# Groups of four transposes of the identity among the up-projections, and conditioning sums that are no longer kept back for the layer norms

## The chip, the cores and the metric

The kernel runs on one core of one Trainium2 chip. Its metric is the device time of one execution in microseconds (us); less is better. The core has a matmul engine (TensorE, PE in the profile, with its weight loads as PEld), two engines for elementwise work that read the matmul results (VectorE, DVE, and ScalarE, ACT), a slower general engine (GpSimd, POOL) and an engine that here only issues transfers (SyncE, SP). Each engine works through its own instructions in order and waits for the others by semaphores.

## What is computed

Two decoder layers over 256 positions of width 2048. Each layer has a token mixer (forgetting attention in layer 0, sliding-window attention in layer 1) and a gated feed-forward network (FFN) with a short convolution. Each sub-layer is scaled, shifted and gated by vectors that come from one conditioning vector `c`:

```python
c_act = jax.nn.silu(c)
for i in range(DEPTH):
    mod = c_act @ ada_w[i] + ada_b[i]
    sh1, sc1, g1, sh2, sc2, g2 = jnp.split(mod[:, None, :], 6, axis=-1)
    h = x * (1.0 + sc1) + sh1
    y = fox_attention(h, ...) if i % 2 == 0 else swa_attention(h, ...)
    x = layer_norm(DEEPNORM_ALPHA * x + (1.0 + g1) * y, ln_mix_g[i], ln_mix_b[i])
    h = x * (1.0 + sc2) + sh2
    y = conv_ffn(h, ffn_w_up[i], ffn_conv_w[i], ffn_conv_b[i], ffn_w_down[i])
    x = layer_norm(DEEPNORM_ALPHA * x + (1.0 + g2) * y, ln_ffn_g[i], ln_ffn_b[i])
```

`conv_ffn` multiplies `h` by `w_up` (2048 x 11264), convolves each channel over three positions, takes `silu(g) * val` of the two halves, and multiplies by `w_down` (5632 x 2048).

## The kernel before

**Weights.** All matrices are f32 in memory. `stream` (L256) walks over one block of 512 columns of a matrix, two chunks of 128 rows at a time: SP fetches a pair (512 KB), ACT rounds it to `wh` (L264), DVE takes the rest `wl = w - wh` (L275), and `go` (L266) issues the matmuls of the pair, then one `tick` of the background work. The activations are split in the same way into `hH` and `hL`, and each product is made of three matmuls: high by high, high by low, low by high.

**Two forms of matmul.** `w_stationary` (L326) is used for the up-projection and for query and key: the weights are the stationary operand and 256 positions stream past them, so each matmul has 256 columns; the profile names its output `ws`. One call has 8 pairs of 24 matmuls, 192 in all, that add up in two PSUM banks. `x_stationary` is used for the rest (`xs` in the profile, 512 columns a matmul).

**The FFN** (`conv_ffn`, L1053) works on the 11 blocks of 512 channels in two stages, `sbs = [(0, 6), (6, NB)]` (L1090): the up-projections of blocks 0 to 5 (two `w_stationary` calls a block, gate half and value half, so 12 calls), the down-projections that they feed, then blocks 6 to 10 (10 calls) and theirs. There are thus four up-projection stages in the two layers.

**Conditioning vectors in the background.** A list (L363) of ten vectors `(layer, v)` is worked off while the matmuls run: (0,3), (0,2), (0,4), (0,5), (1,0), (1,1), (1,3), (1,2), (1,4), (1,5). `ada_vector` (L369) is a generator; `tick` pays for its steps by a rate that is set for each stage. 32 steps each fetch a piece of `ada_w` and add it, times one element of `c`, to the tile `acc` (L391, L393). What then follows depends on the kind of vector:

- Gates (v = 2, 5) first load a bias row into `acc` by a POOL transfer (L381), and end in matmuls against ones (one of 512 columns for each bank) and ACT copies (L405).
- Shifts and scales end in four groups of four transposes of `acc` against the identity (L431), each group followed by four ACT instructions that sum the columns (L435), one group a step.
- The scales (0,4) and (1,4) stand in the table `HELD`. They keep their sums back: `held` collects two functions, and `release` (L444) runs them in the next layer norm, 16 short matmuls of one column against ones and one DVE instruction (L417).

After v = 4 no further vector is begun until `release` has cleared the flag `ada["held"]`.

**The layer norms between sub-layers.** `between` (L1120) runs where one sub-layer's last residual is finished and the next matrix needs the normalised, scaled and transposed `x`. `residual` (L615) has added the gated output and gathered the moments: for each half of the positions DVE prepares the variance (L630), and POOL raises it to the power -1/2 (L631). `between` then ran either `release` or, where nothing was held (the layer norm between the layers), `spin(o, 3)`: three matmuls of the identity by a constant of 384 columns, whose result nobody reads (L504). After that `modulate` (L509) queues the normalisation (L641 on ACT, L643 on DVE), the transposes of `x` (L482) with the scaling that writes `hH` and `hL` (L492 to L497), two further spins, and the first matmuls.

**Order.** The framework orders each engine's instructions by its own plan of when they will be ready; `pin` keeps an instruction in the order of the program. POOL's three instructions around a held layer norm come, in its queue, as L631, L381 (the bias row of the next gate), L631.

Of the kernel before, what the change touches and what calls it, by code (L numbers as in the profile page):

```python
# [17 lines left out]
P = 128  # L18
# [3 lines left out]
KC = D // P  # L22
# [7 lines left out]
DFF = 5632  # L30
# [6 lines left out]
WB = 512  # L37
# [4 lines left out]
def hybrid_trunk(ctx: ExitStack, tc: tile.TileContext, a: dict, out: bass.AP):  # L42
    nc = tc.nc
# [12 lines left out]
    def wtile(name="w"):  # L56
        return wp.tile([P, 2, WB], F32, tag="w", name=name)

    def gtile(name="g"):
        return gp.tile([P, 2, S], F32R, tag="g", name=name)  # L60

    def ttile(name="t"):
        return tp.tile([P, 2 * S], F32, tag="t", name=name)

    def bank(name="sm"):
        return psp.tile([P, 512], F32, tag="ps", name=name)

    def w_banks():
        return [bank("ws").rearrange("p (a s) -> p a s", a=2) for _ in range(2)]
# [4 lines left out]
    def mm(o, lhsT, rhs, start=False, stop=False, **kw):  # L74
        return nc.tensor.matmul(o, lhsT, rhs, start=start, stop=stop, **kw)  # L75

    def pin(ins, on=True):

        if on:
            tc.keep_in_program_order(ins)  # L80

    def split(h, l, src):

        nc.scalar.copy(h, src)  # L84
        nc.vector.tensor_tensor(l, src, f32(h), op=ALU.subtract)
# [14 lines left out]
    ident = cst.tile([P, P], F32, name="ident")  # L100
# [110 lines left out]
    def then(fn, alone=False):  # L211

        if alone:
            lone.add(fn)
        work.append(fn)
        if len(work) == 1 and not ahead[0]:
            settle()
# [3 lines left out]
    def settle(left=0):  # L221
        while work and (ahead[0] > left or not left):
            f = work.pop(0)
            rest(f, *work)
            f()
# [17 lines left out]
    def defer(gen):  # L243

        post.append(gen)

    def run_post():
        for g in list(post):
            if next(g, post) is post:
                post.remove(g)  # L250
# [5 lines left out]
    def stream(wsrc, row0, col, ks, use):  # L256

        for kc in ks[::2]:
            r0 = (row0 + kc) * P
            w = wtile()  # L260
            pin(nc.sync.dma_start(w, wsrc[r0:r0 + 2 * P, col:col + WB].rearrange("(k p) f -> p k f", p=P)), False)
            h = hl.tile([P, 2, WB], F32R, tag="wh", name="wh")
            l = hl.tile([P, 2, WB], F32R, tag="wl", name="wl")
            pin(nc.scalar.copy(h, w), False)  # L264

            def go(kc=kc, h=h, l=l):  # L266
                ahead[0] -= 1
                run_post()
                use(kc, h, l)
                if feeds:  # L270
                    feeds.pop(0)()
                tick()

            def residual_(w=w, h=h, l=l, go=go):
                pin(nc.vector.tensor_tensor(l, w, f32(h), op=ALU.subtract), behind[0] > 0)  # L275
                behind[0] -= 1
                del residuals[go]

            ahead[0] += 1
            weights.add(go)  # L280
            residuals[go] = residual_
            work.append(go)
            settle(2)
# [25 lines left out]
    def w_mm(ps, kc, h, l, last=KC - 1, first=0):  # L309

        for i in range(2):
            for f in range(4):
                o = ps[f // 2][:, f % 2, :]
                wh, wl = h[:, i, f * P:(f + 1) * P], l[:, i, f * P:(f + 1) * P]
                mm(o, wh, hH[:, kc + i, :], start=kc + i == first and f % 2 == 0, skip_group_check=True)
                mm(o, wh, hL[:, kc + i, :], skip_group_check=True)
                mm(o, wl, hH[:, kc + i, :], stop=kc + i == last, skip_group_check=True)
# [5 lines left out]
        stream(wsrc, k0, col, list(range(nk)), use)  # L323
        return ps

    def w_stationary(wsrc, col):  # L326

        ps = w_banks()
        stream(wsrc, 0, col, list(range(KC)), lambda kc, h, l: w_mm(ps, kc, h, l))
        return ps  # L330


# [18 lines left out]
    def drain():  # L351
        while bg["wait"] or bg["run"]:
            step()

    def tick():
        ada_tick()
        if not feeds:
            step()
# [5 lines left out]
    ada = {"gen": None, "debt": 0.0, "rate": 0.0, "gate_free": True}  # L364

    held = []
    HELD = {(0, 4): False, (1, 4): False}

    def ada_vector(l, v):  # L369
        row = v % 3 == 2  # L370
        if (l, v) in HELD and HELD[l, v]:
            q = [cst.tile([P, 512], F32, tag=f"ha{i}", name="ha") for i in range(4)]
# [47 lines left out]

        if (l, v) in HELD:
            held.append((sums, finish))
            ada["held"] = not HELD[l, v]
            ready_cols.add((l, v))
# [19 lines left out]
    def release():  # L444

        for s_, _ in held:
            s_()
        for _, f_ in held:
            f_()
        held.clear()  # L450
        ada["held"] = False
# [15 lines left out]
    def ada_need(l, v):  # L467
        while (l, v) not in cols and (l, v) not in gates and (l, v) not in ready_cols:
            ada_step()
# [34 lines left out]
    def spin(o, n):  # L504

        for _ in range(n):
            pin(mm(o[:, :3 * P], ident, mask.rearrange("p a b -> p (a b)"), start=True, stop=True))
# [545 lines left out]
    def conv_ffn(l):  # L1053
        w_up, w_dn = a["ffn_w_up"][l], a["ffn_w_down"][l]
        NB = DFF // WB
        cw = lambda j, f: ccol[:, l, j, f:f + 1]

        def conv(pf, f):
            u = tp.tile([P, S], F32, tag="u", bufs=3, name="u")
            nc.scalar.activation(u, pf, AF.Identity, bias=cw(CW, f), scale=cw(2, f))  # L1060
            nc.vector.scalar_tensor_tensor(u[:, 1:], pf[:, :S - 1], cw(1, f), u[:, 1:],  # L1061
                                           op0=ALU.mult, op1=ALU.add)
            nc.vector.scalar_tensor_tensor(u[:, 2:], pf[:, :S - 2], cw(0, f), u[:, 2:],  # L1063
                                           op0=ALU.mult, op1=ALU.add)
            return u

        def evac(ps, f0, then):
            u = None
            for f in range(5):
                v = conv(ps[f // 2][:, f % 2, :], f0 + f) if f < 4 else None  # L1070
                if u is not None:
                    then(f - 1, u)
                u = v
                yield
                yield

        def silu(sil):
            def f_(f, u):
                nc.scalar.activation(sil[f // 2][:, (f % 2) * S:(f % 2 + 1) * S], u, AF.Silu)
            return f_  # L1080

        def gated(sil, gT):
            def f_(f, u):
                nc.vector.tensor_tensor(u, u, sil[f // 2][:, (f % 2) * S:(f % 2 + 1) * S], op=ALU.mult)
                g = gtile("gT")
                split(g[:, 0, :], g[:, 1, :], u)
                gT.append(g)
            return f_

        sbs = [(0, 6), (6, NB)]  # L1090
        for si, (b0, b1) in enumerate(sbs):
            gT = []
            then(lambda: ada.update(rate=(0.64, 0.4)[l]))
            for b in range(b0, b1):
                ps = w_stationary(w_up, b * WB)
                sil = [ttile("sil") for _ in range(2)]
                then(lambda ps=ps, b=b, sil=sil: defer(evac(ps, b * 4, silu(sil))))
                ps = w_stationary(w_up, DFF + b * WB)
                then(lambda ps=ps, b=b, sil=sil, gT=gT: defer(evac(ps, DFF // P + b * 4, gated(sil, gT))))

            def stat(kc, t, gT=gT):
                while kc >= len(gT):
                    run_post()
                return gT[kc][:, 0, t * P:(t + 1) * P], gT[kc][:, 1, t * P:(t + 1) * P]

            def ready(si=si):
                if si == 0:
                    drain()
                ada_need(l, 5)
                ada["rate"] = (0.78, 0.4)[l]  # L1110

            then(ready)
            for d in range(D // WB):
                ps = x_stationary(w_dn, d * WB, b0 * 4, (b1 - b0) * 4, stat, (2, 4)[l] if si > 0 and d == D // WB - 1 else 0)
                then(lambda ps=ps, d=d, si=si: defer(residual(ps, d, gates[l, 5], si == len(sbs) - 1)),
                     si > 0 and d == D // WB - 1)
        then(lambda: (flush(), ada.update(gate_free=True)), True)


    def between(l, v, g, b, name, ll):  # L1120

        ada_need(l, v)
        ada_need(l, v + 1)
        o = bank("spin")
        if held:
            release()
        else:
            spin(o, 3)
        modulate(*merged(l, v, g, b, ll), normalise, o)
        behind[0] = 2  # L1130
        later([affine(name, ll)])
# [45 lines left out]
```

## Time and profile before

| what | value |
| --- | --- |
| time before, median of 3 runs | 2258.78 us (2256.72 to 2261.77) |
| profiled execution, its time | 2251.43 us |
| its span (first to last instruction) | 2249.7 us |
| mean granted TensorE clock | 0.989 |
| matmuls on PE | 14903 |
| of these `ws` (weights stationary) | 9984 |
| groups of four transposes of `acc` (L431) | 16 |

The profiled execution lies 7.35 us below the median of the runs. All durations come from it. A matmul's recorded duration is longer than the distance from its start to the next one's start, since matmuls are pipelined; the distances between starts are what counts. In a timeline row, the first number is the start, the second the duration of the row, the last the count of instructions merged into it, and in brackets stands the idle time of the engine and what ended it.

### The profile page before, as it was taken

To read this page: it belongs to the slowest core of one execution; us is meant where nothing else is said; L and a number is where in the kernel's file an instruction comes from. 1 tells how busy PE (TensorE), PEld (TensorE's weight loads), DVE (VectorE), ACT (ScalarE), POOL (GpSimd) and SP (SyncE) were. 2 spreads that over 40 slices of the span, in tenths; PEclk is the share of its full clock that TensorE was granted. 3 is DMA by queue.
4 is the path that set the end of the run, shared out by engine and by line. 5 is a ranking of instruction groups with operands and counts; after the bars stand their busy time and mean duration, and the time that the engine had idled before them with its cause. 6 is when DMAs were issued, how large, how long until landed. Compare 5 with 4: busy or idle time off the path is not lost. (4 is left out here: it accounts for less than half of the span.)

```text
span 2249.7 us, 38317 instructions
## 1 busy us (share of the span) xinstructions
PE 2199.5 (98%) x14903; PEld 2020.0 (90%) x14903; DVE 1793.5 (80%) x2450; ACT 1165.5 (52%) x1833; POOL 22.9 (1%) x52
## 2 busy tenths in 40 slices
PE   6999999999999999999999999999999999999997
PEld 6999888789999888999987888889999888999986
DVE  6979999979979978789799888779787555665656
ACT  3435656455555443655535588655555533454532
POOL 0000000000000000000000000000000000000000
PEclk9999999999999999999999999999999999999998
DMA  9999999959979989799797767559777556555553
GB/s 340 381 342 362 353 354 326 331 197 331 345 248 316 331 282 333 250 314 316 268 326 271 260 236 249 190 171 308 260 263 249 179 192 195 187 188 186 185 193 111
DMA packets 274246, 602.98 MB, mean 268 GB/s; under 512 B 21062, under 2 KB 29960, under 8 KB 273552
## 3 DMA queue, kind: packets, MB, share of 16 engines
q1 hardware_dynamic: 273008, 595.85, 77.2%
q0 software_dynamic: 1056, 4.69, 0.6%
q8 instruction: 116, 1.90, 0.3%
q14 instruction: 66, 0.54, 0.1%
HBM read 598.37 MB, written 2.10 MB: 267 GB/s over the span
## 5 line engine op out<-in xcount | busy, mean ns | idle before, releaser
L264 ACT CAST wh<-w 128x1024 fp32r<-128x1024 f32 x728 | 764.1, 1051 | 826.2 <-PE ws L75 291.8
L75 PE MATMUL ws<-hH,wh 128*128 128x256 f32 x6656 | 1177.6, 281 | 4.6 <-ACT hH L84 2.1
L275 DVE TENSOR_TENSOR wl<-w,wh 128x1024 fp32r<-128x1024 f32 x728 | 886.7, 1221 | 345.8 <-ACT wh L264 336.1
L75 PEld LDWEIGHTS ws<-hH,wh 128*128 128x128 f32 x6656 | 1020.7, 190 | 12.5 <-issue 4.8
L75 PE MATMUL ws<-hH,wl 128*128 128x256 f32 x3328 | 929.4, 281 | 3.6 <-DVE wl L275 3.5
L75 PEld LDWEIGHTS ws<-hH,wl 128*128 128x128 f32 x3328 | 632.5, 191 | 4.9 <-DVE wl L275 4.8
L75 PE MATMUL xs<-wh,gT 128*128 128x512 f32 x1408 | 435.6, 390 | 0.0
L75 PEld LDWEIGHTS xs<-wh,gT 128*128 128x128 f32 x1408 | 264.3, 188 | 54.6
L75 PE MATMUL xs<-wl,gT 128*128 128x512 f32 x704 | 273.9, 389 | 0.0
L75 PE MATMUL xs<-wh,hH 128*128 128x512 f32 x704 | 235.3, 400 | 0.1
L393 DVE SCALAR_TENSOR_TENSOR acc<-wa,cact,acc 128x1024 f32<-128x1024 f32 x180 | 228.1, 1275 | 0.0
L393 DVE SCALAR_TENSOR_TENSOR acc<-wa,cactp,acc 128x1024 f32<-128x1024 f32 x128 | 162.2, 1276 | 0.0
L75 PEld LDWEIGHTS xs<-wl,gT 128*128 128x128 f32 x704 | 132.2, 188 | 27.2
L75 PEld LDWEIGHTS xs<-wh,hH 128*128 128x128 f32 x704 | 131.4, 189 | 27.6 <-issue 1.0
L75 PE MATMUL xs<-wl,hH 128*128 128x512 f32 x352 | 139.5, 397 | 2.0 <-DVE wl L275 2.0
L1060 ACT ACTIVATE u<-ws,ccol 128x256 f32<-128x256 f32 x176 | 96.5, 560 | 59.5 <-PE ws L75 47.7
L75 PE MATMUL xs<-wh,oT 128*128 128x512 f32 x384 | 124.6, 394 | 0.8 <-ACT wh L264 0.7
L1061 DVE SCALAR_TENSOR_TENSOR u<-ws,ccol,u 128x255 f32<-128x255 f32 x176 | 82.5, 477 | 17.9 <-ACT u L1060 17.6
L75 PEld LDWEIGHTS xs<-wh,oT 128*128 128x128 f32 x384 | 72.0, 188 | 15.7 <-ACT wh L264 1.1
L1063 DVE SCALAR_TENSOR_TENSOR u<-ws,ccol,u 128x254 f32<-128x254 f32 x176 | 83.0, 476 | 2.1
L75 PEld LDWEIGHTS xs<-wl,hH 128*128 128x128 f32 x352 | 66.4, 189 | 16.6 <-DVE wl L275 3.6
L562 DVE SCALAR_TENSOR_TENSOR oacc<-wo,cact,oacc 128x1024 f32<-128x1024 f32 (+1 forms) x68 | 73.3, 1078 | 7.8 <-DMA wo<-in_ada_w_dram 6.6
(216 smaller groups left out, 1328.0 us busy)
## 6 DMA issues: line engine op xcount, KB each, us to landing
w<-in_ffn_w_up_dram SPq DMA_DIRECT2D x352, 512.0 KB, 4.7
wa<-in_ada_w_dram SPq DMA_DIRECT2D x320, 512.0 KB, 5.6
w<-in_ffn_w_down_dram SPq DMA_DIRECT2D x176, 512.0 KB, 4.4
w<-in_fox_w_in_dram SPq DMA_DIRECT2D x96, 512.0 KB, 7.0
wo<-in_ada_w_dram SPq DMA_DIRECT2D x48, 512.0 KB, 8.6
w<-in_swa_w_in_dram SPq DMA_DIRECT2D x40, 512.0 KB, 5.5
w<-in_fox_w_o_dram SPq DMA_DIRECT2D x32, 512.0 KB, 6.2
w<-in_swa_w_o_dram SPq DMA_DIRECT2D x32, 512.0 KB, 4.8
```

The costliest lines, as they stand in the source:

```text
L75: return nc.tensor.matmul(o, lhsT, rhs, start=start, stop=stop, **kw)
L264: pin(nc.scalar.copy(h, w), False)
L275: pin(nc.vector.tensor_tensor(l, w, f32(h), op=ALU.subtract), behind[0] > 0)
L393: pin(nc.vector.scalar_tensor_tensor(ac, wo, (cactp if row else cact)[:, k:k + 1], ac, op0=ALU.mult, op1=ALU.add), True)
L562: nc.vector.scalar_tensor_tensor(acc, w[:, k], cact[:, kc:kc + 1], acc, op0=ALU.mult, op1=ALU.add)
L1060: nc.scalar.activation(u, pf, AF.Identity, bias=cw(CW, f), scale=cw(2, f))
L1061: nc.vector.scalar_tensor_tensor(u[:, 1:], pf[:, :S - 1], cw(1, f), u[:, 1:], op0=ALU.mult, op1=ALU.add)
L1063: nc.vector.scalar_tensor_tensor(u[:, 2:], pf[:, :S - 2], cw(0, f), u[:, 2:], op0=ALU.mult, op1=ALU.add)
```

## The change

Two edits. `w_stationary` gets a place `turn_at` at which, between two pairs, PE transposes the identity four times into a PSUM bank that nobody reads. It is used in the second call of block 0 (the value half) and in the first call of block 6, ahead of the third pair (row chunk 4), in each layer: four places. The table `HELD` becomes empty: (0,4) and (1,4) end, as the other shifts and scales do, in transposes of `acc` in the background; `between` always spins.

```diff
+    def turn():
+        o = bank("turn")
+        for j in range(4):
+            pin(nc.tensor.transpose(o[:, j * P:(j + 1) * P], ident, ident))
+
-    def w_stationary(wsrc, col):
+    def w_stationary(wsrc, col, turn_at=-1):
 
         ps = w_banks()
-        stream(wsrc, 0, col, list(range(KC)), lambda kc, h, l: w_mm(ps, kc, h, l))
+
+        def use(kc, h, l):
+            if kc == turn_at:
+                turn()
+            w_mm(ps, kc, h, l)
+
+        stream(wsrc, 0, col, list(range(KC)), use)
         return ps
...
-    HELD = {(0, 4): False, (1, 4): False}
+    HELD = {}
...
-                ps = w_stationary(w_up, b * WB)
+                ps = w_stationary(w_up, b * WB, 4 if b == b0 > 0 else -1)
...
-                ps = w_stationary(w_up, DFF + b * WB)
+                ps = w_stationary(w_up, DFF + b * WB, 4 if b == 0 else -1)
...
         o = bank("spin")
-        if held:
-            release()
-        else:
-            spin(o, 3)
+        release()
+        spin(o, 3)
```

## The prediction

> **What bounds the kernel.** I read the page first, then tables of busy time by window for the `ws` tile alone, then timelines of single engines around the places that the diff touches.
>
> ```profile
> span 2249.7 us, 38317 instructions
> PE 2199.5 (98%) x14903; PEld 2020.0 (90%) x14903; DVE 1793.5 (80%) x2450; ACT 1165.5 (52%) x1833; POOL 22.9 (1%) x52
> ```
>
> PE is never idle for long, so what counts is how fast it gets through its 14903 matmuls. Windows inside the four up-projection stages, on `ws` alone (after PE and PEld come DVE, ACT, the granted clock, DMA share and GB/s):
>
> ```profile
> 524.00:630.00 106.00, 105.30 (x929) 105.10 (x928) 19.87 (x42) 10.93 (x20) 1.00 0.95 337
> 882.00:928.00 46.00, 46.00 (x393) 46.00 (x393) 4.70 (x10) 3.68 (x7) 1.00 0.92 314
> 946.00:1092.00 146.00, 146.00 (x1291) 146.00 (x1290) 26.18 (x56) 15.42 (x28) 1.00 0.89 304
> 1516.00:1736.00 220.00, 220.00 (x1871) 220.00 (x1870) 37.34 (x80) 21.92 (x40) 1.00 0.82 272
> 1902.00:2124.00 222.00, 222.00 (x1887) 222.00 (x1886) 32.73 (x72) 19.72 (x36) 1.00 0.59 187
> ```
>
> Divide time by matmuls: 146.00/1291 = 113.1 ns in the third row, 220.00/1871 = 117.6 in the fourth, 222.00/1887 = 117.6 in the fifth, 46.00/393 = 117.0 in the second (its two edges weigh more), 106.00/929 = 114.1 in the first, which holds a few pauses. The same instruction with the same operands runs at two paces, **fast at 113.1 ns and slow at 117.6**, 4.5 ns apart; the clock is 1.00 in all rows, and PE is busy throughout. Layer 0 runs its first stage fast, its second slow and then fast; layer 1 is slow nearly throughout, though DVE and DMA have less to do there. So it is a condition of PE's own pipeline that lasts once it is entered. What ends it? PE's timeline; `wl` rows come once in three matmuls, so their distance is 0.34 when fast (3 x 113.1), 0.35 to 0.36 when slow (3 x 117.6):
>
> ```profile
> 928.70 0.28 PE L75 MATMUL ws<-hH,wl 128*128 128x256 f32 x1
> 928.82 0.60 PE L431 MATMUL sm<-ident,acc 128*128 128x128 f32 x4
> 929.18 0.48 PE L75 MATMUL ws<-hH,wh 128*128 128x256 f32 x2
> 929.50 0.28 PE L75 MATMUL ws<-hH,wl 128*128 128x256 f32 x1
> 929.61 0.39 PE L75 MATMUL ws<-hH,wh 128*128 128x256 f32 x2
> 929.84 0.28 PE L75 MATMUL ws<-hH,wl 128*128 128x256 f32 x1
> ```
>
> Four transposes of a conditioning vector come between two pairs, and the slow stretch of the window 882 to 928 is over: 0.34 from 929.50 on. Three more groups follow in the fast stretch, the last at 944.1, and it stays fast to 1092:
>
> ```profile
> L431 PE MATMUL sm<-ident,acc x16: 270/272/273, 928.8 to 944.1; 128*128 128x128 f32 x16
> ```
>
> But a group of four transposes of `x` in layer 1 found PE fast (0.34) and left it slow (0.36), and 3 us later another turned it back:
>
> ```profile
> 1508.15 0.28 PE L75 MATMUL ws<-hH,wl 128*128 128x256 f32 x1
> ...
> 1508.49 0.28 PE L75 MATMUL ws<-hH,wl 128*128 128x256 f32 x1
> 1508.61 0.60 PE L482 MATMUL sm<-ident,x 128*128 128x128 f32 x4
> ...
> 1509.28 0.28 PE L75 MATMUL ws<-hH,wl 128*128 128x256 f32 x1
> ...
> 1509.64 0.28 PE L75 MATMUL ws<-hH,wl 128*128 128x256 f32 x1
> ```
>
> I counted the groups of four or more in both FFNs that stand between `ws` matmuls: the slow pace became fast 4 times of 4, the fast pace stayed 7 times of 8. What made layer 1 slow for good was not a group but a pause of 0.1 us between two `wh` matmuls (0.45 from `wl` to `wl`, with 0.34 due):
>
> ```profile
> 1514.95 0.28 PE L75 MATMUL ws<-hH,wl 128*128 128x256 f32 x1
> 1515.06 0.49 PE L75 MATMUL ws<-hH,wh 128*128 128x256 f32 x2
> 1515.40 0.28 PE L75 MATMUL ws<-hH,wl 128*128 128x256 f32 x1
> ```
>
> **The change, part by part.**
>
> *The turns' gain.* A stage of 12 calls has 12 x 192 = 2304 matmuls, one of 10 calls 1920. A turn in the second call's third pair leaves 2304 - 192 - 48 = 2064 behind it, one in the first call's third pair 1920 - 48 = 1872. Layer 1, first stage: all 2064 are slow now (from 1516), gain 2064 x 4.5 = 9.3 us. Second stage: 1872 x 4.5 = 8.4. Layer 0, second stage: slow only until the group at 928.82; from 882 to 928 are 393 matmuls, about 10 more at the start, 48 ahead of the turn, so 393 + 10 - 48 = 355, x 4.5 = 1.6. Layer 0, first stage: fast already, gain 0; here the turn can only lose. Sum **19.3**. Can the rest keep up? The row 946 to 1092 ran fast beside a DMA share of 0.89 with no gap on PE; layer 1 shows 0.82 and 0.59, so DMA covers it.
>
> *The turns' cost.* In the rows at 928, `wl` to `wl` across the group is 0.80 instead of 0.35: 0.45 us. Four turns: **1.8**. They wait for nothing but a bank; the four `ws` banks of two calls leave four of eight.
>
> *The tails of (0,4) and (1,4).* Their last pieces are added here:
>
> ```profile
> 439.06 1.27 DVE L393 SCALAR_TENSOR_TENSOR acc<-wa,cact,acc 128x1024 f32<-128x1024 f32 x1
> 1430.08 1.26 DVE L393 SCALAR_TENSOR_TENSOR acc<-wa,cact,acc 128x1024 f32<-128x1024 f32 x1
> 468.37 0.15 DVE L630 TENSOR_SCALAR mv<-mv 128x1 f32<-128x1 f32 x1
> ```
>
> The layer norm comes 29 us later in layer 0 and 53 in layer 1, so six more steps (a pair of output projection each, under 3 us, at rates of 1.3 and 0.9 steps) end in time. Each vector then has four groups beside `xs` matmuls, at the 0.45 us of a group: eight are 3.6. The `xs` matmuls right after a group may be disturbed: between nothing and one group's time (0.45) a vector, I take 0.2, together **4.0**. The ACT sums (16 a vector) are hidden by ACT's idle half; without that cover, each group would hold the next `wh`.
>
> *The layer norm without held sums.* The layer norm between the layers already has the new form, so its rows are the price list: held form (layer 0), then the spinning one.
>
> ```profile
> 472.38 0.60 POOL L381 DMA_DIRECT2D acc<-in_ada_b_dram  x1 [3.20 <-PE sm L75]
> 473.00 0.57 POOL L631 TENSOR_TENSOR rs<-mv,mhalf 128x1 f32<-128x1 f32 x1
> 477.11 1.20 PE L75 MATMUL ws<-hH,wh 128*128 128x256 f32 x2
> 478.00:480.00 2.00, 2.00 (x11) 2.00 (x11) 2.00 (x4) 0.94 (x2) 0.00 (x0) 0.50 0.00 0
> 1212.63 0.15 DVE L630 TENSOR_SCALAR mv<-mv 128x1 f32<-128x1 f32 x1
> 1215.60 0.55 POOL L631 TENSOR_TENSOR rs<-mv,mhalf 128x1 f32<-128x1 f32 x1 [2.16 <-DVE mv L630]
> 1216.00:1218.00 2.00, 1.22 (x7) 0.95 (x8) 1.82 (x4) 1.49 (x3) 0.14 (x1) 1.00 0.00 0
> 1218.27 0.69 PE L75 MATMUL xs<-wh,hH 128*128 128x512 f32 x1
> ```
>
> In the held form the bias row of the next gate (L381) waits in POOL's queue until the sums have read `acc`, and behind it waits the second L631, on which the normalisation of half the positions hangs: it starts 4.63 us after L630 instead of 2.97, so 1.7 late. Then the clock is down to 0.50 (window 478 to 480) where the spinning form has 1.00 (1216 to 1218). From L630 to the first matmul: 8.74 us held, 5.64 spinning, 3.1 less. With the sums gone, L381 finds `acc` free long before and holds nothing up. If DVE's chain decides, each layer norm gives only the 1.7; if PE does, 3.1 and half of the 2.9 us from 477.11 to 480.00 that ran at half clock, 4.5. I take the 3.1 between the rows, twice (layer 1's held norm has the same order): **6.2**, bounds 3.4 to 9.0. What is late next is `hL` from DVE. SP's queue is not reordered.
>
> *Sum.* -19.3 + 1.8 + 4.0 - 6.2 = **-19.7 us**: 2251.4 becomes 2231.7 on the profiled execution. The three runs lie 7.4 above it at the median. No row says whether that is an offset or a stretch that was fast in the profile and slow in the runs (layer 0's first stage would be 9.3, and the turn would heal it). I carry the offset along: 2258.8 - 19.7 = **2239**; healed, it would be 2232.
>
> The Trainium skill, page "TensorE: Matmul & The Clock Gate", section "Back-to-back issue gap", gives one gap for a warm matmul of 256 columns, 262 cycles or about 109 ns, and no lasting second one. By that the turns could gain nothing, and only their cost would count: it speaks against the change. The rows at 113.1 and 117.6 at full clock disagree with a single gap; the rival it makes is the third below.
>
> **The rivals.**
>
> *One of the three large turns ends slow*, as at 1508.61. Against: 11 good ends of 12. For: what decides is the exact moment at which a group begins, and the second edit shifts all of it. Cost 8.4 to 9.3: about 2248.
>
> *Two end slow*, and the gain is used up: -19.7 + 17.7 to 18.6, about 2257.
>
> *The paces are no matter of transposes*, so that the turns do nothing: the operand places or the stage decide. For: layer 1 is slow as a whole. Against: 928.82, within one stage. Then 1.8 + 4.0 - 6.2 = -0.4: 2258.
>
> *Slower*: transposes of the identity (the same tile as both operands, no wait ahead) always begin at the moment that ends slow. Layer 0's first stage then falls from fast to slow, +9.3, and layer 1 stays: -0.4 + 9.3 = +8.9, 2267.7. It decides from the point at which layer 0 is lost and both layer 1 stages stay slow; one layer 1 stage gained would cancel it.
>
> **How the numbers follow.** Chances: forecast 0.60, one slow end 0.22, two 0.05, turns without effect 0.07, slower 0.06. A measurement of this kernel can tell about 0.2%, 4.5 us. Faster 0.82; within 0.12; slower 0.06. Range: from the healed 2232 less what the layer norms' upper bound adds (9.0 - 6.2 = 2.8) = 2229, to one slow end with the lower bound (2248 + 6.2 - 3.4 = 2251) and the tails' 0.6 more, 2252; two slow ends and the rest are left out (0.18).
>
> **What would show it.** `ws` matmuls per time in layer 1's two stages: 113.1 right, 117.6 wrong. Layer 0's first stage must stay at 113 to 114. L631 in a row without L381's wait, clock 1.00 behind it, first `ws` 5.6 us after L630. Eight more groups of L431 in the output projections, 0.45 each. The forecast is wrong if a pause such as the one at 1515 throws a stage back after its turn, or if the turned stages wait for `wl`.

## The result, and the profile after

| | before | after |
| --- | --- | --- |
| median beside each other, 4 runs each | 2258.03 us (2256.72 to 2261.77) | 2228.39 us (2228.01 to 2231.99) |
| ratio after / before | | 0.9874, 95% interval 0.9852 to 0.9896 |
| profiled execution | 2251.43 us | 2228.63 us |
| its span | 2249.7 us | 2226.8 us |
| mean granted TensorE clock | 0.989 | 0.994 |

The changed kernel is faster by 1.3%. The two profiled executions lie 22.8 us apart where the prediction has 19.7; the medians lie 29.6 apart, because the runs of the kernel before lay some 7 us above its profile and those of the changed kernel lie on theirs.

The top of the page after, and the transposes of `acc` in the view of a line (count, then minimum, median and maximum in ns; line numbers have moved: L431 of before is L442 here, L482 is L493, L630 and L631 are L641 and L642, L393 is L404, L381 is L392):

```profile
span 2226.8 us, 38377 instructions
PE 2175.8 (98%) x14899; PEld 1994.0 (90%) x14899; DVE 1791.6 (80%) x2450; ACT 1176.4 (53%) x1897; POOL 22.8 (1%) x52
```

```profile
L442 PE MATMUL sm<-ident,acc x96: 270/272/301, 253.9 to 1439.8; 128*128 128x128 f32 x96
```

PE has four matmul records fewer (64 of one-column sums are gone; 32 transposes of `acc`, 16 in the turns and 12 spins have come) and is busy 23.7 us less. The eight groups of (0,4) and (1,4) show in the second row: 96 instead of 64.

Windows of the changed kernel on `ws` alone, one in each up-projection stage (columns as in the prediction):

```profile
528.00:628.00 100.00, 100.00 (x885) 100.00 (x884) 18.83 (x40) 10.39 (x19) 1.00 0.96 341
886.00:924.00 38.00, 38.00 (x337) 38.00 (x337) 4.70 (x10) 3.45 (x7) 1.00 0.92 314
1520.00:1722.00 202.00, 202.00 (x1785) 202.00 (x1784) 36.03 (x77) 20.36 (x37) 1.00 0.85 283
1894.00:2101.00 207.00, 207.00 (x1829) 207.00 (x1828) 32.73 (x72) 19.71 (x36) 1.00 0.62 193
```

Time by matmuls gives 113.0, 112.8, 113.2 and 113.2 ns: all four stages run at the fast pace, layer 1 too, where it was 117.6. PE's timeline around the turn of layer 1's second stage:

```profile
1891.28 0.28 PE L75 MATMUL ws<-hH,wl 128*128 128x256 f32 x1
1891.40 0.60 PE L329 MATMUL turn<-ident 128*128 128x128 f32 x4
1891.76 0.48 PE L75 MATMUL ws<-hH,wh 128*128 128x256 f32 x2
1892.08 0.28 PE L75 MATMUL ws<-hH,wl 128*128 128x256 f32 x1
...
1892.42 0.28 PE L75 MATMUL ws<-hH,wl 128*128 128x256 f32 x1
```

From `wl` to `wl` it is 0.80 across the turn (1891.28 to 1892.08, so 0.45 lost) and 0.34 behind it. The layer norm of layer 0, in the timelines of DVE, POOL and PE, and the window right behind the first `ws` matmul (POOL stands in it between ACT and the clock):

```profile
469.99 0.15 DVE L641 TENSOR_SCALAR mv<-mv 128x1 f32<-128x1 f32 x1
470.07 2.10 PE L75 MATMUL spin<-mask,ident 128*128 128x384 f32 x6
472.98 0.55 POOL L642 TENSOR_TENSOR rs<-mv,mhalf 128x1 f32<-128x1 f32 x1 [2.18 <-DVE mv L641]
475.66 0.70 PE L75 MATMUL ws<-hH,wh 128*128 128x256 f32 x2
```

```profile
476.00:478.00 2.00, 2.00 (x19) 2.00 (x18) 2.00 (x6) 2.00 (x5) 0.00 (x0) 1.00 0.00 0
```

No bias row stands before the second power any more: it starts 2.99 us after L641 (4.63 before), the first `ws` follows 5.67 after it (8.74 before), and the clock behind it is 1.00, where it was 0.50.

The first instruction of each stage on PE gives a table of where the time came from:

| stage | before, us | after, us | difference |
| --- | --- | --- | --- |
| up to layer 0's FFN norm | 468.45 | 470.07 | +1.62 |
| that norm | 8.66 | 5.59 | -3.07 |
| layer 0, first up-projection stage | 271.14 | 269.83 | -1.31 |
| layer 0, second stage | 222.51 | 221.39 | -1.12 |
| layer 1's token mixer | 264.78 | 266.48 | +1.70 |
| layer 1's FFN norm | 8.63 | 5.59 | -3.04 |
| layer 1, first stage | 278.48 | 268.69 | -9.79 |
| layer 1, second stage | 226.14 | 218.28 | -7.86 |

### The profile page after: what moved, and what is told of

Read it like the earlier page. It is cut to its first block, busy times and chain, and to the rows that moved or that the text cites. A ratio compares the mean times of both kernels' runs of the same rounds, so it can differ in the third digit from the quotient of the medians.

```text
span 2226.8 us, 38377 instructions
## 1 busy us (share of the span) xinstructions
PE 2175.8 (98%) x14899; PEld 1994.0 (90%) x14899; DVE 1791.6 (80%) x2450; ACT 1176.4 (53%) x1897; POOL 22.8 (1%) x52
## 5 line engine op out<-in xcount | busy, mean ns | idle before, releaser
L75 PE MATMUL ws<-hH,wh 128*128 128x256 f32 x6656 | 1155.3, 279 | 4.5 <-ACT hH L84 2.1
L404 DVE SCALAR_TENSOR_TENSOR acc<-wa,cact,acc 128x1024 f32<-128x1024 f32 x180 | 228.2, 1275 | 0.0
L404 DVE SCALAR_TENSOR_TENSOR acc<-wa,cactp,acc 128x1024 f32<-128x1024 f32 x128 | 162.2, 1276 | 0.0
```

The source lines that it names most:

```text
L404: pin(nc.vector.scalar_tensor_tensor(ac, wo, (cactp if row else cact)[:, k:k + 1], ac, op0=ALU.mult, op1=ALU.add), True)
```

## The experiments

The theory: `ws` matmuls have two lasting paces, and a group of transposes among them nearly always leaves the fast one; so each turn gives what its stage loses to the slow pace, and the layer norms give theirs beside it. The rivals: the pace is drawn anew at every disturbance of the stream, by its moment, so that the second edit can change it as well as the first; or four transposes are nothing special, any interruption does it; and, for the 7 us, either a stage that was fast in the profile of before is slow in most runs, or the executions of before just scatter. Each run's expectation names which of these it was to tell apart. A kernel's times stand beside runs of the kernel before on the same chip; ratios are of those.

**The kernel before, again** (no edit; two more profiles of it stand below).

> The kernel before, unchanged, profiled once more. Theory A (the pace of the up-projection matmuls is a condition that each execution falls into, and layer 0's first stage was fast in the first profile by luck): layer 0's first stage may now be slow, 117.6 ns a matmul instead of 113, and the time then lies near 2258; layer 1's two stages are slow again. Rival B (the 7 us between the first profile and the median of the runs are an offset of another kind): layer 0's first stage fast again, 113 ns, whatever the time.

Measured: 2250.37 us, beside 2254.96 as the median of 11 runs of before (2244.34 to 2261.14). The stages run at the paces of the first profile; the window in layer 1's first:

```profile
1516.00:1735.00 219.00, 219.00 (x1862) 219.00 (x1861) 37.27 (x80) 21.95 (x40) 1.00 0.84 272
```

It is slow at 219.00/1862 = 117.6, and layer 0's first stage is fast: this execution gives no sign of a stage that the turn in layer 0 could heal. *before_third* is the same kernel once more.

> The kernel before, unchanged, profiled a third time. Its runs lie between 2244 and 2261, its first two profiled executions at 2251 and 2250 with layer 0's first stage fast and layer 1's two stages slow. Theory A (the scatter of the runs is scatter of the pace in the two first stages, 9.3 us each): a time away from 2250 goes with a first stage of another pace. Rival B: the same paces whatever the time.

Measured: 2251.47 us, the same paces in every stage.

**The second edit alone**, without any turn:

```diff
-                ps = w_stationary(w_up, b * WB, 4 if b == b0 > 0 else -1)
+                ps = w_stationary(w_up, b * WB, -1)
...
-                ps = w_stationary(w_up, DFF + b * WB, 4 if b == 0 else -1)
+                ps = w_stationary(w_up, DFF + b * WB, -1)
```

> The second edit alone: no sums are held back, no turns. By the prediction's terms: 4.0 us for eight groups of transposes, 6.2 to 9.0 gained in two layer norms, so 2 to 5 us less than before (2253 to 2256), if the up-projections keep their paces. Rival: the different moments at which layer 1's and layer 0's stages begin change their paces as well, and then the time differs from that by 8 to 9 us per stage that is fast instead of slow or the other way. The profile tells which.

Measured: 2237.11 us (2236.42 to 2239.98, 6 runs), ratio 0.9925 (0.9904 to 0.9947), 17.9 us less than before at the median; by the prediction's terms it is 4.0 - 6.2, 2.2 less. Its windows in layer 1's two stages:

```profile
1512.00:1724.00 212.00, 212.00 (x1873) 212.00 (x1872) 37.21 (x80) 22.01 (x40) 1.00 0.86 282
1890.00:2110.00 220.00, 220.00 (x1870) 220.00 (x1869) 32.79 (x72) 19.76 (x36) 1.00 0.64 187
```

The first stage runs at 113.2 ns without a turn, the second at 117.6 as before. So the second edit alone had already given the first stage's 9 us. Where the two kernels part is the pause that the prediction found at 1515. It is a wait for the last piece of `hL`, which DVE writes in L85. In the kernel with the second edit alone:

```profile
1510.27 0.68 DVE L85 TENSOR_TENSOR hH<-t,hH 128x512 fp32r<-128x512 f32 x1
1510.78 0.61 PE L75 MATMUL ws<-hH,wh 128*128 128x256 f32 x2
1511.22 0.28 PE L75 MATMUL ws<-hH,wl 128*128 128x256 f32 x1
...
1511.57 0.28 PE L75 MATMUL ws<-hH,wl 128*128 128x256 f32 x1
```

And in the kernel before, ahead of the rows that the prediction shows:

```profile
1514.44 0.68 DVE L85 TENSOR_TENSOR hH<-t,hH 128x512 fp32r<-128x512 f32 x1
```

L85 ends at 1510.95 and 1515.12; the weights of the second matmul in the 0.61 row are loaded from 1511.00 on, those of the second in the 0.49 row from 1515.17 on (rows of PEld): each about 0.05 after L85's end. The row is 0.22 longer than the 0.39 of one that waits for nothing, against 0.10 before: PE comes to this point earlier, as DVE counts. Behind the longer pause PE was fast here (0.35, then 0.34 from `wl` to `wl`), behind the shorter one it was slow.

**The turns alone**, the sums held as before:

```diff
-    HELD = {}
+    HELD = {(0, 4): False, (1, 4): False}
...
-        release()
-        spin(o, 3)
+        if held:
+            release()
+        else:
+            spin(o, 3)
```

> The first edit alone: four turns, the sums still held back. Theory A: layer 1's stages and layer 0's second fast, 17.5 us net, and layer 0's first stage fast in every run, which gives back the 7 us of the runs over the first profile as well: 2234 (2232 to 2237). Rival B (the 7 us have nothing to do with pace): 2258 - 17.5 = 2240.

Measured: 2236.09 us (2232.54 to 2245.26, 6 runs), ratio 0.9923 (0.9899 to 0.9946). Its profiled span is 2231.8, against 2247.8 to 2249.7 in the four profiles of before: 16.0 to 17.9 less, with 17.5 worked out in the prediction. One of the six runs, 2245.26, lies some 8 us above the next (2237.69); it has no profile, so whether a stage was slow in it is open. PE's timeline at the wait for L85, then the two windows of layer 1:

```profile
1513.66 0.49 PE L75 MATMUL ws<-hH,wh 128*128 128x256 f32 x2
1513.99 0.28 PE L75 MATMUL ws<-hH,wl 128*128 128x256 f32 x1
...
1514.35 0.28 PE L75 MATMUL ws<-hH,wl 128*128 128x256 f32 x1
```

```profile
1524.00:1727.00 203.00, 203.00 (x1793) 203.00 (x1793) 36.42 (x78) 20.40 (x37) 1.00 0.86 284
1899.00:2106.00 207.00, 207.00 (x1829) 207.00 (x1828) 32.74 (x72) 19.76 (x36) 1.00 0.67 193
```

With the sums held the pause is 0.10 again and PE slow behind it (0.36 from 1513.99 on); the turn then ends that, and both stages are fast behind their turns. The two parts alone give 17.9 and 18.9 us against the median of 2254.96, some 36.7 together, but the changed kernel at 2228 lies only about 27 below it: layer 1's first stage, 9.3, is in both.

**All but layer 0's first turn:**

```diff
-                ps = w_stationary(w_up, DFF + b * WB, 4 if b == 0 else -1)
+                ps = w_stationary(w_up, DFF + b * WB, 4 if b == 0 and l > 0 else -1)
```

> The changed kernel without the turn in layer 0's first up-projection; the other three stay. Theory A: that stage takes its pace from what the layer norm's transposes leave; where it is slow the time is 9 us above the changed kernel (2237), where it is fast 0.45 us below (2228); the runs may scatter between the two. Rival B: always 2228, since a turn in a stage that is fast gives nothing.

Measured: 2229.98 us (2227.05 to 2231.05, 6 runs), ratio 0.989 (0.987 to 0.991); the profiled span is 2226.7, as with the turn. Layer 0's first stage in two windows:

```profile
500.00:524.00 24.00, 24.00 (x206) 24.00 (x205) 2.84 (x6) 2.67 (x5) 1.00 0.90 308
527.00:628.00 101.00, 101.00 (x894) 101.00 (x892) 19.09 (x41) 10.37 (x19) 1.00 0.97 342
```

It is slow at first (116.5 ns) and fast (113.0) behind a wait for `wl` at 524.7, which ends the slow stretch by itself. So this turn gives next to nothing, as the prediction had it: what it could heal lasts only to 524.7.

**Turns in the second stages only**, and then **all but layer 1's first turn**, two kernels without a turn in layer 1's first stage:

```diff
-                ps = w_stationary(w_up, DFF + b * WB, 4 if b == 0 else -1)
+                ps = w_stationary(w_up, DFF + b * WB, -1)
```

> The changed kernel with turns only in the second up-projection stage of each layer (first call of block 6), none in the first stages. Theory (without held sums both first stages end up fast by themselves after the last pauses at their start, as in the profile of the second edit alone; what the turns win is layer 1's second stage, 8.4, and layer 0's, 1.6): the two turns left out only saved nothing and cost 0.45 each, so the time is that of the changed kernel less 0 to 1 us, 2227 to 2229. Rival (layer 1's first stage needs its turn in most executions, the one profile of the second edit alone was luck): up to 9 us more in the runs, 2232 to 2237.

```diff
-                ps = w_stationary(w_up, DFF + b * WB, 4 if b == 0 else -1)
+                ps = w_stationary(w_up, DFF + b * WB, 4 if b == 0 and l == 0 else -1)
```

> The changed kernel without the turn in layer 1's first up-projection; the three others stay. Theory (this turn is what kept the runs without it from splitting into 2226 to 2228 and 2236 to 2238): the runs split again, some at 2227, some 9 us higher, and in the profile the stage is fast where the time is low and slow where it is high. Rival (the split came from layer 0's first stage, which has its turn here): all runs between 2227 and 2232.

Measured: the first 2232.41 us, ratio 0.9916 (0.9888 to 0.9945), in two heaps, 2225.76 to 2228.30 and 2236.52 to 2238.16, three runs each; the second 2229.13 us, ratio 0.9929 (0.9906 to 0.9951), five runs from 2225.76 to 2230.11 and one at 2237.81. Both profiled executions are from the lower heap, and their first stage in layer 1 is fast, row by row:

```profile
1512.00:1722.00 210.00, 210.00 (x1856) 210.00 (x1855) 37.45 (x80) 21.50 (x40) 1.00 0.86 283
```

```profile
1514.00:1724.00 210.00, 210.00 (x1855) 210.00 (x1854) 37.37 (x80) 21.37 (x39) 1.00 0.86 283
```

The middles of the heaps lie 9 to 10 us apart, about what that stage is worth (9.3). Over all runs with the sums in the background and a turn there (the changed kernel twice, and two of its variants), none of 20 lies higher than 2232. Of the 18 runs without that turn 4 lie some 9 us above the others of their kernel: three of six, one of six, and none of the six with the second edit alone. So the stage looks like a draw that the turn there settles, on few runs. That the higher runs are those with a slow first stage fits the size; no profile of a higher run was caught, so it is argued, not shown.

**Plain matmuls for the transposes**, the same four products with no transpose:

```diff
-            pin(nc.tensor.transpose(o[:, j * P:(j + 1) * P], ident, ident))
+            pin(mm(o[:, j * P:(j + 1) * P], ident, ident, start=True, stop=True))
```

> The changed kernel with four ordinary f32 matmuls of the identity by the identity (128 columns) at the four places, instead of four transposes. Theory A (any interruption of the even stream that shifts the moment can change the pace): layer 1's second stage is fast behind it as well, 113 ns, and the time is that of the changed kernel within 2 us (the four matmuls may cost a little more). Rival B (it is the transposes that set it): the stage stays at 117.6 ns, 8 us more, and layer 0's second stage stays slow to its first group of L442.

Measured: 2227.95 us (2226.31 to 2231.36, 4 runs), ratio 0.9902 (0.9868 to 0.9935). PE's timeline in layer 1's second stage, and the window behind it:

```profile
1888.36 0.28 PE L75 MATMUL ws<-hH,wl 128*128 128x256 f32 x1
1888.48 1.05 PE L75 MATMUL turn<-ident 128*128 128x128 f32 x8
...
1889.61 0.28 PE L75 MATMUL ws<-hH,wl 128*128 128x256 f32 x1
```

```profile
1892.00:2098.00 206.00, 206.00 (x1820) 206.00 (x1819) 32.80 (x72) 19.80 (x36) 1.00 0.67 193
```

Four f32 matmuls show as eight, take longer, and end the slow pace as well (206.00/1820 = 113.2). It is not the transpose that counts.

**Groups of one, two, three and four** in turn, in nearly every call:

```diff
+    calls = [0]
...
-        for j in range(4):
+        n = (1, 2, 3, 4)[calls[0] % 4]
+        calls[0] += 1
+        for j in range(n):
...
-                ps = w_stationary(w_up, b * WB, 4 if b == b0 > 0 else -1)
+                ps = w_stationary(w_up, b * WB, 4 if b > 0 else -1)
...
-                ps = w_stationary(w_up, DFF + b * WB, 4 if b == 0 else -1)
+                ps = w_stationary(w_up, DFF + b * WB, 4)
```

> The changed kernel with a group of transposes of the identity in every call of the up-projections except the first one of each layer's block 0, ahead of the third pair, of 1, 2, 3, 4 transposes in turn: 42 groups, 105 transposes, of which 16 stand in the changed kernel, so about 11 us more if all stretches stay fast. Theory A (the pace after a group depends on the moment at which the group ends, not on the number four): groups of every length sometimes leave the stream slow and sometimes fast, and the same length does both. Rival B (four is a count that always ends fast): every group of four leaves it at 113 ns, and the shorter ones leave some stretches at 117.6.

Measured: 2256.29 us, one run, no faster than before. Two of its groups of four stand at 576.06 and at 668.61; windows on `ws` ahead of and behind each:

```profile
555.00:575.00 20.00, 20.00 (x172) 20.00 (x171) 3.84 (x8) 2.27 (x5) 1.00 0.98 347
578.00:597.00 19.00, 19.00 (x170) 19.00 (x169) 3.47 (x8) 2.24 (x4) 1.00 0.89 301
655.00:668.00 13.00, 13.00 (x117) 13.00 (x116) 1.44 (x3) 1.58 (x3) 1.00 0.81 267
670.00:690.00 20.00, 20.00 (x172) 20.00 (x171) 3.46 (x8) 2.24 (x4) 1.00 0.87 294
```

The first group finds PE slow (20.00/172 = 116.3 ns; short windows lose up to 2 ns at their edges) and leaves it fast (19.00/170 = 111.8). The second, the same four instructions, finds it fast (13.00/117 = 111.1) and leaves it slow (20.00/172 = 116.3). Single transposes turned the pace both ways as well. So four is no special count: many groups throw the pace about, and few, placed where the stage is known to be slow, help.

What goes with the outcome is a matter of nanoseconds. Over all 14 profiles, groups of four transposes in the up-projection stages that found PE slow left it fast 54 times of 57. Of the 113 that found it fast 20 left it slow, and these can nearly be told by the `wl` matmul ahead of the group: its record was 282 ns in all 20, and 277, 278, 280 or 284 in 92 of the 93 that stayed fast. The one exception, 282 ns and fast behind it, is a turn of the change itself: layer 1's first, at 1515.01 in the second profile of the changed kernel (*after_again*). The group of that experiment at 668.61, and layer 1's turn in the changed kernel, in the view of a line (minimum, median, maximum):

```profile
L75 PE MATMUL ws<-hH,wl x1: 282/282/282, 668.5 to 668.5; 128*128 128x256 f32 x1
```

```profile
L75 PE MATMUL ws<-hH,wl x1: 280/280/280, 1517.2 to 1517.2; 128*128 128x256 f32 x1
```

A few ns in one record sort 112 of 113; what in PE they stand for, no run shows.

Nor does any interruption do it. The gates' sums also fall into these stages, one matmul of 512 columns (two records) at a time. One at 1738.47 in the kernel before found PE slow and left it slow: `wl` starts at 1737.99, 1738.35, 1739.56 and 1739.91, thus 0.36, 1.21 across the sum, and 0.35. Over the 14 profiles 18 such sums found PE slow and 93 found it fast, and none of the 111 changed the pace, though this one cost 0.86 us, about twice a group of four transposes and nearly as much as the four plain matmuls above (1888.36 to 1889.61, 1.25 where 0.35 is due).

**The changed kernel again.**

> The changed kernel, unchanged, once more beside fresh runs of before. Its runs so far lie between 2228 and 2232. Theory (with a turn ahead of each long stretch, every stage is fast in every execution): 2227 to 2232 again, no run near 2237. Rival (the pace is drawn anew each time): one or two runs of six 9 us higher.

Measured: 2228.22 us (2225.80 to 2230.81, 6 runs), ratio 0.9924 (0.9903 to 0.9946), all four stages fast. Beside it the 11 runs of before fell into two heaps, 2240.22 to 2242.89 (5) and 2246.33 to 2253.40 (6). So the ratio moves with the kernel before, not with the changed one, which lies within 2226 to 2232 in all ten runs.

**Sums held, spins behind them**, in the kernel before:

```diff
-        if held:
-            release()
-        else:
-            spin(o, 3)
+        release()
+        spin(o, 3)
```

> The kernel before, with the sums held back as they were, but with the three spins after them in every layer norm (2.1 us more of PE work, no turns). It tells POOL's wait from the clock. Theory (of the 3.1 us from L630 to the first matmul that the spinning form is shorter, 1.7 come from POOL's queue and the rest from the half clock): the clock stays at 1.00, L631 still waits for L381, and the first ws matmul starts about 7.3 us after L630. Rival (the clock is all of it): about 5.6 to 6. Rival (POOL is all of it): 8.7, as before. The matmuls right behind it run at 0.12 us in the first two cases, 0.21 in the last.

Measured: 2241.15 us, one run. The layer norm of layer 0 in the timeline, and two windows in and behind it (POOL again ahead of the clock):

```profile
469.18 0.15 DVE L630 TENSOR_SCALAR mv<-mv 128x1 f32<-128x1 f32 x1
469.26 3.63 PE L75 MATMUL sm<-ones,acc 128*128 128x1 f32 x32
472.75 3.32 PE L75 MATMUL spin<-mask,ident 128*128 128x384 f32 x6
473.19 0.60 POOL L381 DMA_DIRECT2D acc<-in_ada_b_dram  x1 [3.20 <-PE sm L75]
473.81 0.57 POOL L631 TENSOR_TENSOR rs<-mv,mhalf 128x1 f32<-128x1 f32 x1
478.32 0.70 PE L75 MATMUL ws<-hH,wh 128*128 128x256 f32 x2
```

```profile
474.00:476.00 2.00, 2.00 (x5) 0.97 (x4) 1.59 (x4) 0.00 (x0) 0.38 (x1) 0.50 0.77 246
478.00:480.00 2.00, 2.00 (x16) 1.74 (x15) 2.00 (x6) 1.83 (x5) 0.00 (x0) 1.00 0.00 0
```

Now PE is busy without a gap from 469.26 on, and still the clock falls to 0.50 behind the 3.63 us of one-column sums; the three spins (six records) take 3.32 us instead of 2.10 in the changed kernel. The spins bring it back to 1.00 by the first `ws`, but that comes 9.14 us after L630, later than the 8.74 of before. None of the three times expected came. It is thus the one-column matmuls that lower the clock, not an idle PE, and L631 waits behind L381 as before. All profiles agree: with held sums the clock fell to 0.50 in both FFN layer norms of all six, and without them in neither norm of the eight others, although PE idles there too (0.49 and 0.86 us ahead of the transposes of `x` in the changed kernel's layer 0). How much of the 3.1 us POOL's queue is worth by itself, with the power 1.64 us earlier (4.63 to 2.99), stays open. That the run is 2241 all the same fits layer 1's first stage, which this once is fast from 1514.7 on.

**The kernel before, a fourth profile**, to catch its lower heap.

> The kernel before, unchanged, profiled a fourth time. In the last comparison its eleven runs fell into two heaps, five at 2240 to 2243 and six at 2246 to 2253, and all profiled executions so far belong to the higher one, with layer 1's first stage slow. Theory (the heaps differ by the pace of layer 1's first stage): if this one lies near 2241 or 2242 that stage is fast in it, if it lies near 2250 it is slow. Rival: the same pace in both heaps.

Measured: 2249.59 us, of the upper heap again, layer 1's first stage slow. Its pause for L85 is of the longer kind (a row of 0.61), and PE is slow behind it all the same: the length of the pause alone doesn't decide. What the lower heap is stays open.

## Why the prediction was right, and where it was not

*The two paces and the turns.* Right in place and size. The three terms that were worked out as 9.3, 8.4 and 1.6 less 0.45 for each turn show in the table as 9.79, 7.86 and 1.12, the first with some of the layer norm's clock in it; the turns alone took 16.0 to 17.9 off the span, with 17.5 worked out. Layer 0's first turn gave nothing, as said. The rivals with one or two slow ends did not show in any of the 20 runs; only with the sums held did one run of six (2245.26) lie as high as one slow end would put it; those with turns that do nothing, or that end slow always, are refuted by the windows after. But one reason behind the turns was too simple: a group of transposes does not repair the pace as such. Plain matmuls, a wait for `wl` or one transpose do it too, the gates' sums never did, and 20 of 113 groups that met a fast PE spoiled it. "11 good ends of 12" was a fair count of something that the moment decides.

*What the prediction missed.* It took layer 1's first stage as slow unless a turn ends it. With the sums gone, that stage starts otherwise, and was fast before its turn came (at 1517.28), in this profile also behind the pause for L85, from 1509.6 on; the second edit alone was worth 17.9 us at the median, not 2.2. The sum came out because the turn then had only to keep what was there: two causes for one term. The prediction named the shift of moments by the second edit as a danger; here it was a gain.

The Trainium skill, page "TensorE: Matmul & The Clock Gate", section "Back-to-back issue gap", has one gap for a warm matmul of 256 columns (262 cycles, about 109 ns). The section calls it the gap of an isolated matmul; for streams of weight loads and matmuls, as here, it has figures for 128 and 512 columns alone, so it doesn't forecast this stream as directly as the prediction took it to. By a single gap no turn could gain. The rows show two, 113.2 and 117.6, with a clock of 1.00 in both, and the runs decided for the rows.

*The layer norms.* The mechanism was right, the term too small. Each norm became 3.07 and 3.04 shorter, with 3.1 predicted. But the matmuls behind it were gained too: layer 0's first stage without a turn takes 269.59 us in the kernel with the second edit alone (476.87 to 746.46) and 271.14 before, 1.55 less, since it no longer begins at half clock. In layer 1 the 21st `ws` matmul starts 3.34 us after the first, and 4.36 before: 1.0 of the 9.79 belongs here. Together some 8.6, not 6.2, and inside the bounds of 3.4 and 9.0. The step that failed is "I take the 3.1 between the rows": it ended the account at the first `ws`, though the half clock went on behind it; the upper bound had that part in it. That the clock falls because of the one-column sums and not because PE idles, only the run with sums and spins showed.

*The tails.* 4.0 predicted, 1.62 + 1.70 = 3.3 measured. The 1.70 holds: layer 1's token mixer takes 264.8 us in all four profiles of before, 266.5 and 266.4 in the two of the changed kernel. It is four groups at 0.45 with nothing for their neighbours. The 1.62 is weaker: the start of layer 0's first stage scatters by about 2 us between profiles of one kernel (475.27 to 477.64 before, 475.66 and 473.41 after).

*The sum and the offset.* -22.8 on the profiles, with -19.7 predicted: the layer norms gave 2.4 more and the tails cost 0.7 less. The rest of the distance from 2239 to 2228, which is the very low end of the prediction's range (2229 by its working), is the 7.4 that was carried along. It belonged to the kernel before, whose runs spread over 21 us (2240 to 2262) while the changed kernel's spread over 6. Beside other runs of before, with a median of 2246.33, the same changed kernel was only 18.1 us faster: how near -19.7 comes to the measured difference depends on the runs that it is set against. The other reading in the prediction, a first stage of layer 0 that a turn heals, gave nearly the right number for a wrong reason: without that turn the kernel is as fast. The spread of before may be the draw in layer 1's first stage: its step fits, and the run of the held sums with spins, fast there, lay at 2241. But all four profiles of the kernel before had that stage slow and none came from the lower heap, so it isn't shown. The runs near 2260 stay unexplained.

## What to carry to other kernels

Divide time by instructions for one form in each stage: when the same matmul has two paces at a full clock and no waits, the pace is a state that lasts, and four short matmuls where the stage is known to be slow can end it (54 times of 57 here); put few of them, since a group that meets a fast stretch can spoil it (20 of 113). When an edit shifts the moments of a whole stage, draw that stage's pace anew in the forecast, and measure the two parts of a change alone: here their gains overlap by 9 us. And follow a wait's price past the instruction that waited: some 30% of the layer norms' gain (2.5 of 8.6 us) lay in matmuls that came after them.

## What the runs showed of the hardware that was not expected

- The same `ws` matmul at 113.2 or 117.6 ns apart with the clock at 1.00, for hundreds of us; it changed at interruptions of 0.1 to 0.9 us, but not at each. At the wait for L85 in layer 1, PE was slow behind a pause of 0.10 us 4 times of 4, and fast behind one of 0.22 us 7 times of 8.
- Between the two stand pauses of 0.11 us, behind which PE was fast twice of twice. The size of the interruption alone doesn't sort the cases: one pause of 0.22 us left PE slow, and sums of 0.86 us changed nothing. That the exact moment decides is the reading that is left; the 282 ns ahead of a group of four, right 112 times of 113, speaks for it and doesn't prove it.
- The one-column sums of a held vector (16 matmuls, 32 records), 3.63 us without a gap, took the granted clock from 1.00 down to 0.50, and three spins of 384 columns (six records) brought it back. The Trainium skill, page "TensorE: Matmul & The Clock Gate", Part 1, ties the clock to how busy PE has been over a window of about 3.4 us; the length of the sums is near that window, but the trace agrees only if such matmuls count as next to no work there, although it shows PE busy.
